# Loading the weights of a one-core network in units of 1 MB with 8192 bytes per row instead of 512 KB with 4096

## The chip, the cores and the metric

The kernel runs on one core of a Trainium2 chip. The metric is the device time of one execution in microseconds (us), taken from the start to the end of the program on the chip. One core has a matrix engine (PE), a vector engine (DVE), an activation engine (ACT), a general engine (POOL), a sequencer that only issues transfers (SP), and 16 DMA engines that move data between the chip's memory (HBM) and the core's own memory (SBUF).

## What is computed

Two networks follow one another on 256 tokens of width 1024, all in float32. The first has two layers: a convolution block and a differential attention, each followed by a mixture of 16 experts of which every token takes 2. The second is one layer: a state-space mixer beside a stick-breaking attention, and a gated feed-forward layer. Cut to the part that the weight loads serve:

```python
def grouped_moe(x, router_w, router_bias, w_gate, w_up, w_down):
    ...
    def step(acc, ew):
        g_e, wg_e, wu_e, wd_e = ew
        h = jax.nn.silu(x2 @ wg_e) * (x2 @ wu_e)
        return acc + (h @ wd_e) * g_e[:, None].astype(x2.dtype), None

    out, _ = lax.scan(step, jnp.zeros_like(x2), (gates.T, w_gate, w_up, w_down))

def first_block(...):
    for l in range(DEPTH):                      # DEPTH = 2
        mix = conformer_conv(...) if l < N_A else diff_attention(...)
        x = layer_norm(ALPHA * x + mix, ln_mix_g[l], ln_mix_b[l])
        ffn = grouped_moe(x, router_w, router_bias, moe_w_gate[l], moe_w_up[l], moe_w_down[l])
        x = layer_norm(ALPHA * x + ffn, ln_ffn_g[l], ln_ffn_b[l])
```

Each layer's experts hold 16 x 3 matrices of 1024 x 512, 96 MB in float32. With the other matrices the program reads some 300 MB of weights, each once.

## The kernel before

The program runs in five phases, one after the other: **A** the convolution block (`pw1`, 8 units of weights, the convolution, `pw2`, 4 units), **B** the first mixture of experts (`moe0`, 96 units), **C** the attention (`wk`, `wq`, `wv`, `wo`, 16 units), **D** the second mixture (`moe1`, 96 units), **E** the second network (`win` 22, `wout` 8, `wup` 22, `wdown` 11 units). A unit is 1 MB: 128 rows (one to each partition of SBUF) of 2048 floats.

**The order of the loads.** All weights go through one list, `plan`, made by `order` (L276) in the order of use, and through one issuing queue, SP's. An entry of the list is a half unit: 128 rows of 1024 floats, 512 KB, rows of 4096 bytes cut from the unit's 8192. `issue` (L299) takes the next entry, takes a slot from a ring and issues the DMA (L304). There are five rings of 512 KB slots, opened as SBUF comes free: `ring1` 6 slots, `ring2` 16, `ring3` 4 and `ring5` 8 (both of `RING3`), `ring4` 4, 38 slots or 19 MB in all. In phase E only `ring1` is left. `half` (L323) hands the next loaded half to the code that uses it and notes its ring; `flush` (L317) issues the next loads once more than `LAG` used halves are noted. An issued load still waits on SP until the last reader of its slot has finished. It waits too until the DMA that last used its completion counter has landed: the program has eight such counters, DMAHW0 to DMAHW7, given in turn to the DMAs of SP and ACT, so that at most eight transfers are under way.

**Phases A, C, E.** `split_half` (L356) splits each half in two: ACT copies it rounded into `wh` (L361), and POOL or DVE, in turn, subtract to get `wl` (L370). `mm3` multiplies three times (L375 to L377). A slot is free when the half's `wl` is done.

**Phases B, D.** The experts go in pairs, p = 0 to 7, 12 units each (gate 4, up 4, down 4). The matmuls read the loaded halves directly: `col2` (L803) issues two matmuls that stand side by side in the array, one for each expert of the pair (L805 and L806). `up` and the down loop (L897) take, for each step, the half `s` of unit `i` and the half `s` of unit `i + 1` (`two_halves`, L808), the first of one expert and the second of the other. `pairs` in `order` lists the halves so: (i, 0), (i+1, 0), (i, 1), (i+1, 1). After the pair p = 0, the code asks whether any expert has got more tokens than its slots hold (`overflow`, L971, the branch at L981); on these inputs none has. All engines, SP too, pass that branch, and at its end SP waits on all eight completion counters before it issues the next load.

**The small transfers of other queues.** At the end of phase D, ACT's queue issues the constants of phase E: `al` and `db` (L1377), `cols_e`, `cst_e`, `cst_eb` (L250) and the meta tokens into `hT` (L1239, pieces of 64 bytes). DVE's first work in phase E is `wdh` (L1303), cast from `cols_e`; the last normalisation of phase D (`v_f` L426, `y` L434) is queued behind it on DVE, and PE's transposes `fm_hT` (L446) need that `y`. PE fills the time with 21 matmuls on a constant (`warm`, L353). Later, in the mixer, SP writes a row to HBM (`acsd`, L1424) and reads it back spread over the partitions (`acs`, L1531) for DVE's `E` (L1538).

Of the kernel before, what the change touches and what calls it, by code (L numbers as in the profile page):

```python
# [9 lines left out]
F32 = mybir.dt.float32  # L10
# [7 lines left out]
P = 128  # L18
# [23 lines left out]
FT = DFF // P  # L42
XT = 12
NEG = -1e30
RING2 = 16
RING3 = (4, 8)
RING4 = 4

W = dict(start=16, a=16, l0=16, lg=9, pos=(4, 6), f0=22, f1=22, l1=18, mix=20)
CONV_PE = (4, 5, 6, 7)  # L50
# [4 lines left out]
LO_DVE = 4  # L55
LO_BOTH = 4
XH_ACT = (1, 2, 3)
LAGS = (6, 2, 2)
M0 = NMETA - 2
NM = L - M0  # L60

# [70 lines left out]
def pack(I):  # L132
    g = {k: np.asarray(v) for k, v in I.items()}
    a = {}
# [4 lines left out]
    c = {}  # L139
# [57 lines left out]
    for l in range(DEPTH):  # L197
        us = []
        for p in range(NE // 2):
            for nm in ("moe_w_gate", "moe_w_up", "moe_w_down"):  # L200
                ua = [units_q(g[nm][l][2 * p + s]) for s in range(2)]
                for h in range(2):
                    us.append(ua[0][h])
                    us.append(ua[1][h])
        a[f"moe{l}"] = np.stack(us)
    order = [0, 4, 1, 5, 2, 6, 3, 7]
    a["wk"] = units_p(g["w_kv"][:, :D], order)
# [15 lines left out]
class Net:  # L223
# [51 lines left out]

    def order(self, phases):  # L276
        plan = []
        add = lambda nm, *ix: plan.extend((nm, i, s) for i in ix for s in range(2))
        pairs = lambda nm: plan.extend((nm, i + e, s) for i in range(0, 96, 2) for s in range(2) for e in range(2))
        if "A" in phases:  # L280
            add("pw1", *range(8))
            add("pw2", *range(4))
        if "B" in phases:
            pairs("moe0")
        if "C" in phases:
            for nm, *ix in (("wk", 0), ("wq", 0), ("wv", 0, 1), ("wk", 1), ("wq", 1), ("wk", 2), ("wq", 2), ("wv", 2, 3), ("wk", 3), ("wq", 3), ("wo", 0, 1, 2, 3)):
                add(nm, *ix)
        if "D" in phases:
            pairs("moe1")
        if "E" in phases:  # L290
            add("win", *range(22))
            add("wout", *range(8))
            add("wup", 0)
            for u in range(FT // 2):
                add("wup", *range(2 * u + 1, min(2 * u + 3, FT)))
                add("wdown", u)
        self.plan = plan

    def issue(self, ring):  # L299
        if self.issued == len(self.plan):  # L300
            return
        nm, i, s = self.plan[self.issued]
        t = self.rings[ring].tile([P, 1024], F32, tag="unit", name=f"u_{nm}_{i}_{s}")
        self.nc.sync.dma_start(t, self.I[nm][i][:, s * 1024:(s + 1) * 1024])  # L304
        self.issued += 1
        self.live.append((nm, i, s, t, ring))
        if self.issued == 1 and nm == "pw1":
            self.first_loads(lambda: self.issue(ring))

    def open_ring(self, ctx, ring, n):  # L310
        self.flush()
# [8 lines left out]
            if r in self.rings and self.issued < len(self.plan) and self.retire.get(r, self.plan[self.issued][0]) == self.plan[self.issued][0]:  # L320
                self.issue(r)

    def half(self, nm, i, s):  # L323
        if not self.live:
            self.flush()
        a, b, c, t, ring = self.live.pop(0)
        assert (a, b, c) == (nm, i, s), (a, b, c, nm, i, s)
        self.used.append(ring)
        self.flush(self.LAG)
        return t  # L330

    def unit(self, nm, i):
        return [self.half(nm, i, s) for s in range(2)]

    def after(self, ins, prev):
        self.tc.add_manual_dep(ins.ins, prev.ins.name, mybir.DependencyInfo(mybir.DependencyClass.NoSync, mybir.DependencyReason.DATA), reason="order")
# [117 lines left out]
    def build(self, phases="ABCDE"):  # L454
        tc, nc = self.tc, self.nc
        self.order(phases)
        with ExitStack() as ctx:
# [14 lines left out]
                self.open_a(late, early)  # L472
            else:
                self.first_loads()
            self.open_ring(ctx, "ring1", 6)
            c2 = ctx.enter_context(ExitStack())
            if phases != "E":
                self.open_ring(c2, "ring2", RING2)
# [17 lines left out]
            if "D" in phases:  # L496
                xs, src = self.moe(1, xs, "mix_g1", "mix_b1", ["ring4", "ring5", "ring3", "ring2"], rows(1))
# [225 lines left out]
    def moe(self, l, n, gname, bname, last_rings, rows):  # L723
        nc = self.nc
        with ExitStack() as ctx:
# [79 lines left out]
                nc.tensor.matmul(ps[0:64], a, ra, start=first, stop=last)  # L805
                self.upped = nc.tensor.matmul(ps[64:128], b, rb, start=first, stop=last)  # L806

            def two_halves(i, s, k):  # L808
                return [self.half(f"moe{l}", i + e, s).rearrange("p (k n) -> p k n", k=k) for e in range(2)]

            def up(p, q, xe, name):
                ps = self.bank(f"{name}{l}{p}")
                for h in range(2):
                    for s in range(2):
                        wa, wb = two_halves(12 * p + 4 * q + 2 * h, s, 2)
                        for kk in range(2):
                            k = 4 * h + 2 * s + kk
                            o = P * (p % 2)
                            col2(ps, xe[:, k, o:o + 64], xe[:, k, o + 64:o + 128], wa[:, kk], wb[:, kk], k == 0, k == KT - 1)
                return ps  # L820
# [34 lines left out]
            for p in range(8):  # L855
# [38 lines left out]
                py = [self.bank(f"py{l}{p}{nh}") for nh in range(2)]  # L894
                for hh in range(2):
                    for kk in range(2):
                        wa, wb = two_halves(12 * p + 8 + 2 * hh, kk, 1)  # L897
                        k = 2 * hh + kk
                        for nh in range(2):
                            s = slice(nh * 512, nh * 512 + 512)  # L900
                            col2(py[nh], hT[:, k, 0:64], hT[:, k, 64:128], wa[:, 0, s], wb[:, 0, s], k == 0, k == 3)
# [69 lines left out]
    def overflow(self, l, b1, xnh, xnl, identr, gname, bname, posm, gates, nmax, xacc):  # L971
        nc, tc = self.nc, self.tc
        units = self.I[f"moe{l}"]

        def chunk(p, i, kk):
            w = self.yy.tile([P, D], F32, tag="yl", name="ovw")[:, :512]
            nc.sync.dma_start(w, units[bass.ds(p * 12 + i, 1), :, kk * 512:(kk + 1) * 512].rearrange("o p n -> p (o n)"))
            return w
# [867 lines left out]
```

## Time and profile before

| | |
|---|---|
| time, median of 3 runs (lowest, highest) | 1196.36 us (1191.97, 1198.35) |
| the profiled execution, its own time | 1195.35 us |
| its span, first to last instruction | 1193.6 us |
| PE, busy share of the span | 96% |
| DVE, ACT, POOL, busy share | 55%, 41%, 27% |
| weight loads on SP's queue | 303.84 MB, 85080 packets |
| PE's granted clock over the span | 0.99 |

The page divides the span into 40 slices of 30 us and gives for each the busy share of every engine and the GB/s that the DMAs moved. Waits are listed by the waiting instruction and by what released it. A matmul's end is modelled from its start, so a matmul that was held up inside the array shows as a longer or as a merged row and counts as busy.

### The profile page before, as it was taken

How to read it: one execution, taken by the hardware profiler on the slowest of the kernel's cores; microseconds unless marked ns; L12 is line 12 of the kernel's file. 1: busy time of each engine (PE TensorE's matmuls, PEld its weight loads, DVE VectorE, ACT ScalarE, POOL GpSimd, SP SyncE). 2: the span in 40 equal slices, each digit the busy share in tenths (PEclk: the TensorE clock that was granted, in tenths of full speed). 3: DMA queues.
4: the chain of work that ended last, by engine and by line, in shares of the span. 5: the costliest groups of instructions: out<-in, count | busy, mean ns of one | idle time of the engine just before them, and what ended most of it. 6: DMA issues, size and time to landing. Idle time of an engine off the chain costs nothing.

```text
span 1193.6 us, 19220 instructions
## 1 busy us (share of the span) xinstructions
PE 1146.7 (96%) x7362; PEld 825.0 (69%) x7370; DVE 652.1 (55%) x1287; ACT 492.1 (41%) x923; POOL 328.1 (27%) x211
## 2 busy tenths in 40 slices
PE   8999899999999999899999998989999998999996
PEld 7998534344335898544344435988999997999996
DVE  5998622222215785632222215974998768655655
ACT  4786311011114575411010114554667666444443
POOL 5872000000002433000000003652222675444443
PEclk8999999999999999999999999999999999999998
DMA  9957498999999866778999996444433463555551
GB/s 350 404 124 223 185 339 330 409 409 409 409 388 347 319 221 214 264 296 328 409 409 409 409 409 210 142 146 150 128 110 101 150 186 116 194 187 180 187 192 46
DMA packets 90214, 311.52 MB, mean 261 GB/s; under 512 B 11215, under 2 KB 14208, under 8 KB 90112
## 3 DMA queue, kind: packets, MB, share of 16 engines
q1 hardware_dynamic: 85080, 303.84, 68.8%
q10 hardware_dynamic: 5032, 6.33, 2.4%
q8 instruction: 62, 1.02, 0.3%
q14 instruction: 40, 0.33, 0.1%
HBM read 307.50 MB, written 2.64 MB: 260 GB/s over the span
## 4 chain that ended last, share of the span: by engine, by line
PE 40%; DVE 8%; ACT 2%; issue 1%; DMA 1%; POOL 1%; ACTq 0%; POOLq 0%; DVEq 0%; SPq 0%
PE py L805 4%; PE up L376 4%; PE up L377 4%; PE up L375 4%; PE pg L805 3%; PE pu L805 3%; PE pdn L377 2%; PE pdn L376 2%; PE pdn L375 2%; DVE E L1538 2%; PE dwin L375 1%; PE dwin L377 1%; PE dwin L376 1%; PE dwout L377 1%; PE dwout L376 1%; PE dwout L375 1%
## 5 line engine op out<-in xcount | busy, mean ns | idle before, releaser
L805 PE MATMUL py<-u_moe,hT 128*64 128x512 f32 x256 | 113.5, 595 | 3.6 <-ACT hT L889 2.6
L805 PE MATMUL pg<-u_moe,xe 128*64 128x512 f32 x256 | 114.6, 594 | 0.0
L806 PE MATMUL py<-u_moe,hT 128*64 128x512 f32 x256 | 114.2, 597 | 0.0
L806 PE MATMUL pu<-u_moe,xe 128*64 128x512 f32 x256 | 113.2, 594 | 0.6 <-DMA u_moe<-in_moe 0.6
L805 PE MATMUL pu<-u_moe,xe 128*64 128x512 f32 x256 | 113.7, 594 | 0.0
L806 PE MATMUL pg<-u_moe,xe 128*64 128x512 f32 x256 | 113.2, 594 | 0.0
L375 PE MATMUL dwin<-xih,wh 128*128 128x272 f32 (+1 forms) x352 | 104.1, 296 | 0.0
L376 PE MATMUL dwin<-xil,wh 128*128 128x272 f32 (+1 forms) x352 | 101.4, 288 | 1.1 <-DVE xil L1279 1.1
L377 PE MATMUL dwin<-xih,wl 128*128 128x272 f32 (+1 forms) x352 | 100.9, 287 | 1.6 <-POOL wl L370 1.6
L376 PE MATMUL up<-fxl,wh 128*128 128x258 f32 (+1 forms) x352 | 99.7, 283 | 1.6 <-DVE fxl L1719 1.6
L874 DVE TENSOR_TENSOR h<-h,pu 128x512 f32<-128x512 f32 x16 | 11.0, 687 | 165.1 <-PE pu L806 151.4
L375 PE MATMUL up<-fxh,wh 128*128 128x258 f32 (+1 forms) x352 | 99.7, 283 | 0.8 <-ACT fxh L1718 0.8
L377 PE MATMUL up<-fxh,wl 128*128 128x258 f32 (+1 forms) x352 | 99.7, 283 | 0.0
L907 DVE SCALAR_TENSOR_TENSOR yl<-py,gc,yh 128x512 fp32r<-128x512 f32 x32 | 23.6, 749 | 108.4 <-ACT yh L906 101.0
L805 PEld LDWEIGHTS py<-u_moe,hT 128*64 128x64 f32 x256 | 33.7, 137 | 71.0 <-issue 61.6
L370 POOL TENSOR_TENSOR wl<-u_win,wh 128x1024 fp32r<-128x1024 f32 x25 | 62.0, 2478 | 63.4 <-ACT wh L361 60.7
L805 PEld LDWEIGHTS pg<-u_moe,xe 128*64 128x64 f32 x256 | 34.1, 137 | 59.0 <-issue 54.2
L370 POOL TENSOR_TENSOR wl<-u_wup,wh 128x1024 fp32r<-128x1024 f32 x22 | 53.6, 2435 | 63.4 <-ACT wh L361 37.4
L805 PEld LDWEIGHTS pu<-u_moe,xe 128*64 128x64 f32 x256 | 34.1, 137 | 52.1 <-issue 50.9
L376 PEld LDWEIGHTS up<-fxl,wh 128*128 128x128 f32 x352 | 66.9, 190 | 2.5 <-DVE fxl L1719 1.8
L375 PEld LDWEIGHTS up<-fxh,wh 128*128 128x128 f32 x352 | 66.9, 190 | 2.0 <-ACT fxh L1718 1.3
L376 PEld LDWEIGHTS dwin<-xil,wh 128*128 128x128 f32 x352 | 66.3, 188 | 2.0 <-DVE xil L1279 1.9
(537 smaller groups left out, 3237.5 us busy)
## 6 DMA issues: line engine op xcount, KB each, us to landing
u_moe<-in_moe SPq DMA_DIRECT2D x384, 512.0 KB, 10.2
u_win<-in_win SPq DMA_DIRECT2D x44, 512.0 KB, 3.6
u_wup<-in_wup SPq DMA_DIRECT2D x44, 512.0 KB, 4.0
u_pw<-in_pw SPq DMA_DIRECT2D x24, 512.0 KB, 10.2
u_wdown<-in_wdown SPq DMA_DIRECT2D x22, 512.0 KB, 4.0
u_wout<-in_wout SPq DMA_DIRECT2D x16, 512.0 KB, 3.8
u_wk<-in_wk SPq DMA_DIRECT2D x8, 512.0 KB, 7.3
u_wq<-in_wq SPq DMA_DIRECT2D x8, 512.0 KB, 9.3
```

The source lines that it names most:

```text
L370: eng.tensor_tensor(l, w, h.bitcast(F32), ALU.subtract)
L375: mm(ps, lh, rh, start=first, stop=False)
L376: mm(ps, lh, rl, start=False, stop=False)
L377: mm(ps, ll, rh, start=False, stop=last)
L805: nc.tensor.matmul(ps[0:64], a, ra, start=first, stop=last)
L806: self.upped = nc.tensor.matmul(ps[64:128], b, rb, start=first, stop=last)
L874: nc.vector.tensor_tensor(h, h, pu, ALU.mult)
L907: nc.vector.scalar_tensor_tensor(yl[:, s], py[nh], gc, yh[:, s].bitcast(F32), op0=ALU.mult, op1=ALU.subtract)
L1538: nc.vector.tensor_scalar(E[:, q:q + w], a[:, i, q:q + w], nA[:, c, h:h + 1], 0.0, op0=ALU.add, op1=ALU.min)
```

## The change

- A load is one DMA of a whole unit, 1 MB, 128 rows of 8192 bytes. `issue` takes a tile of [128, 2, 1024]; `unit` hands out its two halves.
- The rings have half as many slots of twice the size: 3, 8, 2 and 4, 2, so 19 slots and the same 19 MB. `LAGS` goes from (6, 2, 2) to (3, 1, 1), in units now.
- The expert weights are packed anew in HBM: a unit holds one step's half of one expert and, in the same row, that of the other. `moe0` and `moe1` are then listed plainly, unit 0 to 95, and `both` replaces `two_halves`.
- The very first unit is still loaded in two DMAs with the input `xT` between them; the second unit of `pw1` now follows at once, ahead of `cols_a` and the other constants.
- The overflow code, which does not run, finds its pieces at the new places.

```diff
-LAGS = (6, 2, 2)
+LAGS = (3, 1, 1)
...
                 for h in range(2):
-                    us.append(ua[0][h])
-                    us.append(ua[1][h])
+                    for c in (slice(0, 1024), slice(1024, 2048)):
+                        us.append(np.concatenate([ua[0][h][:, c], ua[1][h][:, c]], 1))
...
-        nm, i, s = self.plan[self.issued]
-        t = self.rings[ring].tile([P, 1024], F32, tag="unit", name=f"u_{nm}_{i}_{s}")
-        self.nc.sync.dma_start(t, self.I[nm][i][:, s * 1024:(s + 1) * 1024])
+        nm, i = self.plan[self.issued]
+        t = self.rings[ring].tile([P, 2, 1024], F32, tag="unit", name=f"u_{nm}_{i}")
+        src = self.I[nm][i].rearrange("p (s n) -> p s n", s=2)
         self.issued += 1
-        self.live.append((nm, i, s, t, ring))
+        self.live.append((nm, i, t, ring))
         if self.issued == 1 and nm == "pw1":
-            self.first_loads(lambda: self.issue(ring))
+            self.nc.sync.dma_start(t[:, 0], src[:, 0])
+            self.first_loads(lambda: (self.nc.sync.dma_start(t[:, 1], src[:, 1]), self.issue(ring)))
+        else:
+            self.nc.sync.dma_start(t, src)
...
-            def two_halves(i, s, k):
-                return [self.half(f"moe{l}", i + e, s).rearrange("p (k n) -> p k n", k=k) for e in range(2)]
+            def both(i, k):
+                return [w.rearrange("p (k n) -> p k n", k=k) for w in self.unit(f"moe{l}", i)]
```

At the branch on SP's queue (L981 before, L982 after), half a unit moves. Before, in the list of `moe0`:

```order
L304 DMA u_moe0_30_0_2056<-in_moe0 128x1024
L304 DMA u_moe0_31_0_2058<-in_moe0 128x1024
L304 DMA u_moe0_30_1_2064<-in_moe0 128x1024
L981 COMPARE_AND_BRANCH
...
L981 UNCONDITIONAL_BRANCH
L304 DMA u_moe0_31_1_2066<-in_moe0 128x1024
L304 DMA u_moe0_32_0_2072<-in_moe0 128x1024
```

and after:

```order
L311 DMA u_moe0_30_1973<-in_moe0 128x2048
L311 DMA u_moe0_31_1979<-in_moe0 128x2048
L982 COMPARE_AND_BRANCH
...
L982 UNCONDITIONAL_BRANCH
L311 DMA u_moe0_32_1985<-in_moe0 128x2048
L311 DMA u_moe0_33_1991<-in_moe0 128x2048
```

The last load ahead of the branch was the third of four halves of a pair of units; now the pair is whole, and the branch stands between two pairs.

On SP's queue in phase E, around the write of `acsd` and its read `acs0`, before:

```order
L304 DMA u_win_7_1_7640<-in_win 128x1024
L304 DMA u_win_8_0_7726<-in_win 128x1024
L1424 DMA acsd_7589<-acs_row_7587 16x258
L1531 DMA acs0_8152<-acsd_7589 128x516
L304 DMA u_win_8_1_7728<-in_win 128x1024
L1531 DMA acs1_8182<-acsd_7589 128x516
```

and after:

```order
L311 DMA u_win_7_7185<-in_win 128x2048
L1425 DMA acsd_7136<-acs_row_7134 16x258
L1532 DMA acs0_7687<-acsd_7136 128x516
L311 DMA u_win_8_7271<-in_win 128x2048
L1532 DMA acs1_7717<-acsd_7136 128x516
```

The half of unit 8 that stood ahead of `acsd` now goes with the other, behind `acs0`.

On ACT in phase A, where `sg0` is the gate of the first result and `dg0` are diagonal matrices for the convolution, made from `wch` and `wcl`, before:

```order
L361 ACTIVATE wh_232<-u_pw1_0_1_120 128x1024
L604 ACTIVATE dg0_0_386<-cst_m_126,wch_197 128x128 x3
L604 ACTIVATE dg0_0_386<-cst_m_126,wcl_198 128x128 x4
L361 ACTIVATE wh_265<-u_pw1_1_0_132 128x1024
L645 ACTIVATE sg0_261<-pw1_0_207,cols_a_122 128x256
L361 ACTIVATE wh_294<-u_pw1_1_1_134 128x1024
```

and after:

```order
L361 ACTIVATE wh_211<-u_pw1_0_114 128x1024
L361 ACTIVATE wh_244<-u_pw1_1_121 128x1024
L361 ACTIVATE wh_273<-u_pw1_1_121 128x1024
L645 ACTIVATE sg0_240<-pw1_0_186,cols_a_123 128x256
L604 ACTIVATE dg0_0_365<-cst_m_127,wch_176 128x128 x3
L604 ACTIVATE dg0_0_365<-cst_m_127,wcl_177 128x128 x4
```

The seven `dg0` copies moved from before the second unit's splits to behind `sg0`.

## Rows read from the trace of the kernel before

**Rows 1.** The page: GB/s moved in 40 slices of 30 us

```profile
GB/s 350 404 124 223 185 339 330 409 409 409 409 388 347 319 221 214 264 296 328 409 409 409 409 409 210 142 146 150 128 110 101 150 186 116 194 187 180 187 192 46
```

**Rows 2.** Waits, all engines: who waited for what, us in total, times, longest

```profile
PEld py L805 <- DMA u_moe<-in_moe: 5.5, 14, 1.9
DVE wdh L1303 <- DMA cols_e<-in_cols_e: 2.9, 1, 2.9
DVE E L1538 <- DMA acs<-acsd: 2.3, 1, 2.3
```

**Rows 3.** Waits of SP's queue, same columns

```profile
SPq L304 <- DMA u_moe<-in_moe: 258.9, 279, 3.9
SPq L981 <- SPq L981: 21.4, 6, 10.7
```

**Rows 4.** Timeline of PE, end of phase B: start, us, what, [idle before it]

```profile
344.27 0.64 PE L806 MATMUL pu<-u_moe,xe 128*64 128x512 f32 x1
...
349.51 1.07 PE L805 MATMUL pu<-u_moe,xe 128*64 128x512 f32 x2
...
359.00 1.88 PE L805 MATMUL py<-u_moe,hT 128*64 128x512 f32 x4
...
363.41 1.50 PE L805 MATMUL py<-u_moe,hT 128*64 128x512 f32 x3 [1.04 <-DMA u_moe<-in_moe]
...
366.62 1.52 PE L828 MATMUL sum<-yh,sT 128*128 128x512 f32 x4
```

**Rows 5.** Timeline of PE, the same stretch of phase D

```profile
705.40 0.64 PE L806 MATMUL pu<-u_moe,xe 128*64 128x512 f32 x1
...
723.01 1.37 PE L828 MATMUL sum<-yh,sT 128*128 128x512 f32 x4
```

**Rows 6.** Stretches: PE, PEld, DVE, ACT, POOL busy, PEclk, DMA share, GB/s

```profile
180.00:210.00 30.00, 27.76 (x142) 12.47 (x138) 7.03 (x12) 4.54 (x9) 0.00 (x0) 1.00 0.87 330
210.00:240.00 30.00, 30.00 (x154) 11.28 (x155) 6.66 (x14) 2.92 (x5) 0.00 (x0) 1.00 1.03 409
330.00:360.00 30.00, 29.42 (x127) 11.04 (x124) 4.20 (x8) 3.54 (x5) 0.00 (x0) 1.00 1.01 379
```

**Rows 7.** One DMA queue, whole span and 937.1 to 938.1 us: packets, MB, share

```profile
q14 instruction: 40, 0.33, 0.1%
...
q14 instruction: 1, 0.01, 1.9%
```

**Rows 8.** Timelines of ACT's queue, DVE and PE, from phase D to E

```profile
724.27 0.34 ACTq L250 DMA_DIRECT2D cols_e<-in_cols_e  x1
...
727.25 0.21 DVE L424 BATCH_NORM_AGGREGATE mv_f<-st_f 128x2 f32<-128x12 f32 x1
730.34 0.23 DVE L1303 CAST wdh<-cols_e 128x128 fp32r<-128x128 f32 x1 [2.88 <-DMA cols_e<-in_cols_e]
...
725.15 4.96 PE L353 MATMUL warm<-warm_b 128*128 128x512 bf16 x21
733.05 3.42 PE L446 MATMUL fm_hT<-cst_m,y 128*128 128x128 f32 x16 [2.94 <-DVE y L434]
```

**Rows 9.** A stretch within that change of phase, columns as in rows 6

```profile
726.00:728.00 2.00, 2.00 (x11) 0.88 (x10) 1.43 (x5) 0.00 (x0) 0.00 (x0) 1.00 0.94 175
```

**Rows 10.** Phase A: what the engines waited for from 4 to 30 us

```profile
DVE hp L646 <- ACT sg L645: 3.6, 1, 3.6
PE pw L377 <- DVE wl L368: 0.3, 1, 0.3
```

**Rows 11.** DMA issues (KB each, us to landing), and one refill in phase E

```profile
u_moe<-in_moe SPq DMA_DIRECT2D x384, 512.0 KB, 10.2
u_wup<-in_wup SPq DMA_DIRECT2D x44, 512.0 KB, 4.0
...
1036.70 0.33 SPq L304 DMA_DIRECT2D u_wup<-in_wup  x1
...
1045.64 1.06 ACT L361 ACTIVATE wh<-u_wup 128x1024 fp32r<-128x1024 f32 x1 [1.71 <-PE up L376]
```

More of the change, by code (lines that the diff above doesn't have):

```diff
@@ L44 @@
 NEG = -1e30
-RING2 = 16
-RING3 = (4, 8)
-RING4 = 4
+RING1 = 3
+RING2 = 8
+RING3 = (2, 4)
+RING4 = 2
 W = dict(start=16, a=16, l0=16, lg=9, pos=(4, 6), f0=22, f1=22, l1=18, mix=20)
@@ L277, in order @@
         plan = []
-        add = lambda nm, *ix: plan.extend((nm, i, s) for i in ix for s in range(2))
-        pairs = lambda nm: plan.extend((nm, i + e, s) for i in range(0, 96, 2) for s in range(2) for e in range(2))
+        add = lambda nm, *ix: plan.extend((nm, i) for i in ix)
         if "A" in phases:
@@ L283, in order @@
         if "B" in phases:
-            pairs("moe0")
+            add("moe0", *range(96))
         if "C" in phases:
@@ L288, in order @@
         if "D" in phases:
-            pairs("moe1")
+            add("moe1", *range(96))
         if "E" in phases:
@@ L321, in flush, with unit @@
                 self.issue(r)
-    def half(self, nm, i, s):
+    def unit(self, nm, i):
         if not self.live:
             self.flush()
-        a, b, c, t, ring = self.live.pop(0)
-        assert (a, b, c) == (nm, i, s), (a, b, c, nm, i, s)
+        a, b, t, ring = self.live.pop(0)
+        assert (a, b) == (nm, i), (a, b, nm, i)
         self.used.append(ring)
         self.flush(self.LAG)
-        return t
-    def unit(self, nm, i):
-        return [self.half(nm, i, s) for s in range(2)]
+        return [t[:, s] for s in range(2)]
     def after(self, ins, prev):
@@ L474, in build @@
                 self.first_loads()
-            self.open_ring(ctx, "ring1", 6)
+            self.open_ring(ctx, "ring1", RING1)
             c2 = ctx.enter_context(ExitStack())
@@ L814, in up @@
                     for s in range(2):
-                        wa, wb = two_halves(12 * p + 4 * q + 2 * h, s, 2)
+                        wa, wb = both(12 * p + 4 * q + 2 * h + s, 2)
                         for kk in range(2):
@@ L896, in moe @@
                     for kk in range(2):
-                        wa, wb = two_halves(12 * p + 8 + 2 * hh, kk, 1)
+                        wa, wb = both(12 * p + 8 + 2 * hh + kk, 1)
                         k = 2 * hh + kk
@@ L975, in chunk @@
         def chunk(p, i, kk):
+            i, kk = i - i % 2 + kk // 2, i % 2 * 2 + kk % 2
             w = self.yy.tile([P, D], F32, tag="yl", name="ovw")[:, :512]
```

## The prediction

> **What bounds the kernel now.** I read the GB/s by slice first, then the waits, then the timelines where the waits sit. PE is busy nearly all the time, so an edit to loads can only pay where PE stands for a load. The slices show two plateaus at exactly 409 GB/s, the greater part of the two expert phases, and far less in the second network [rows 1]. On the plateau the DMA engines are the limit: SP is held back 279 times by a load that has not landed [rows 3], and their busy share is full [rows 6]. So the expert phases live on the 19 MB that were loaded ahead, and run out of them at their end.
>
> The list of waits hides this. It charges PE's weight loads only 5.5 us in 14 pieces [rows 2]. But a matmul's end is modelled, so a late load shows as one long merged row: 1.88 us for four matmuls, and so on [rows 4]. The honest measure is the same work twice. From one given `pu` matmul of the last expert pair to its first `sum`, phase B takes 366.62 - 344.27 = 22.35 us [rows 4] and phase D 723.01 - 705.40 = 17.61 us [rows 5]. **Phase B loses 4.74 us at its end** to late loads. In phase D the loads come just in time.
>
> The second place is the change from phase D to E. The last loads of `moe1` and the first three units of `win` are still under way when ACT asks for `cols_e` at 724.27. DVE is free at 727.25 + 0.21 = 727.46, waits for `cols_e` until 730.34, and holds the last normalisation behind it; PE then stands for 2.94 us before `fm_hT` [rows 8]. In the middle of that stretch the DMA engines are 94% busy and move 175 GB/s [rows 9]: they are full, and with small pieces.
>
> **The change, part by part.**
>
> *Rows of 8192 bytes.* On the plateau each of 16 engines moves 409 / 16 = 25.6 GB/s, so 8192 bytes, now two packets, take 0.320 us. The trace has a few packets of 0.33 MB / 40 = 8.2 KB on another queue; one of them, alone in a window of 1 us, took 1.9% of 16 engine-microseconds, 0.304 us, which rounding leaves between 0.296 and 0.312 [rows 7]. With nothing else, that is a gain of 2.5 to 7.5%; with something added for the update of the counter, or if it is HBM or the path that limits, it is nothing. I bound it by 0 and 5% and take 3%, since the packet on record is nearest in kind.
>
> What 3% gives: 64 units are loaded after the branch in each expert phase, 64 x 1.049 MB / 409 GB/s = 164 us, of which 3% are 4.9 us. Some 13 units load back to back ahead of the branch, which adds 1.0 us. So the last unit lands about **5.9 us earlier**, and each per cent is worth 2.0 us. Phase B needs 4.74, that is 2.4%. I enter **-4.7**. In phase D nothing is lost now but a tenth here or there: **-0.2**.
>
> *The branch.* In the 30 us that hold it, 330 GB/s were moved and not 409 [rows 6]: 79 x 30 / 409 = 5.8 us of loading are lost, since SP waits 10.7 us for eight counters [rows 3] and the queue then refills from nothing. After the change the same eight counters are awaited, the data ahead of them is one half unit more, and the refill is as long. The half unit, 0.5 MB / 409 = 1.3 us, only moves from behind the branch to ahead of it. Entry 0; bounds 1.3 us of lead either way, which in phase B is a gain or loss of at most that. The same holds for twice as much data under way: on a plateau that is already full a longer queue adds no rate.
>
> *From D to E.* If all weight loads are 5.9 us ahead, the first three `win` units, which ended near 730 us, end near 724, when `cols_e` is only being asked for. Then `wdh` starts when DVE is free, 2.88 us earlier. PE's `warm` ends at 725.15 + 4.96 = 730.11, and `fm_hT` would come at 733.05 - 2.88 = 730.17, so no new floor is in the way [rows 8]. What is late next is `cst_e`, asked for right after `cols_e` and needed by DVE within 1.5 us of `wdh`; for it I keep 0.2 back. Entry **-2.7**, bounds 0 and -2.9.
>
> What the trace shows there is that small pieces beside weight packets make slow progress. [...]
>
> *Issue order in phase E.* Ahead of `acsd` one half unit fewer is issued, so `acs0`, for which DVE waits 2.3 us [rows 2], meets less traffic. PE has other matmuls there; entry **-0.3**, bounds 0 and -1.0.
>
> *Whole units in the ring of three.* A unit's slot comes free when its second half is split, and its first split now needs all of it. In the tightest refill the second half is issued at 1036.70 and the unit's first split begins at 1045.64, 8.94 us later [rows 11]. A half lands in 4.0 us there [rows 11]; eight more packets per engine at 0.16 us make 5.3 (an estimate from these rows). That leaves 3.6 us, so entry 0. [...]
>
> *Phase A.* The second unit overtakes `cols_a`, so that ACT's splits come sooner and the `dg0` copies after `sg0`. PE's listed waits there are tenths: 0.3 us for a `wl` [rows 10]. The copies now stand between `sg0` and the third unit's splits and can delay those by as much. Entry 0, bounds -0.5 and +0.5. The halved count of issues on SP costs nothing: SP has been waiting for landings, not for its own issuing.
>
> **The sum**, against the profiled execution's 1195.35 us: -4.7 - 0.2 - 2.7 - 0.3 = -7.9, so 1187.4. The profiled execution stands 1.0 us below the median of the runs, 1196.36; the same ratio gives 1188.4. I say 1188.
>
> **The rivals.**
>
> *The rate does not rise.* For it: the plateau is so flat that something other than packets may set it. Against it: in the trace a packet of twice the size takes less than twice the time. Then phase B's end and the wait for `cols_e` stay, and only -0.3 and the tenths of phase A remain: 1195, and to 1197 if the constants' pieces wait longer between larger packets: `cols_e` has 128 rows, 8 to an engine, and 8 x 0.15 us make 1.2.
>
> *Half of it.* The lead comes, but the wait at the change of phase passes from `cols_e` to `cst_e` or the meta tokens, or the lead is 1.5% and covers 3 us of phase B. One term or the other falls: 1190 to 1192.
>
> *Slower: the ring of three starves.* Place: the splits of phase E, a slot freed only as a whole. It decides from a landing time of 8.94 us on. For it: the expert loads took 10.2 us from issue to landing [rows 11], which is over that. Against it: they had seven others ahead of them, and in phase E hardly half of the rate is used [rows 1]. If a unit took 10.2 us, each of the ten repeated groups of three units would start 10.2 - 8.9 = 1.3 us late, 13 us in all: 1188 + 13 = 1201.
>
> **How the numbers follow.** The forecast gets 0.55: the packet on record carries it. The flat rate gets 0.27, half of it 0.08, the starving ring 0.10. A measurement of this kernel can tell about 0.5% from no change, 6 us, so the bound lies at 1190.4. The forecast's bounds, -10.5 to -6, fall on the faster side; of the half case a quarter does: 0.57 faster. The flat rate and the rest of the half case are within the bound: 0.33. Slower: 0.10. The range runs from 1185, all terms at their good ends, to 1196.5, which takes in most of the flat-rate case and leaves out the starving ring.
>
> **What would show it.** Slices of the plateaus at about 421 GB/s, with packets of 8192 bytes on the weights' queue (half as many of them). The stretch from the `pu` matmul to `sum` in phase B at 17.6 us, as in phase D. `wdh` no longer waiting for `cols_e`, and `fm_hT` right behind `warm`. No new wait of ACT's splits for `u_wup` or `u_wdown`. If the slices stay at 409, the step on packets is wrong and with it the two main terms; if they rise and the stretch stays at 22 us, it was not the loads that held PE there.

## The result and the profile after

| | before | after |
|---|---|---|
| time, median of 4 runs (lowest, highest) | 1196.15 us (1191.97, 1198.35) | 1176.18 us (1173.67, 1177.86) |
| the profiled execution, its span | 1195.35, 1193.6 us | 1173.67, 1171.9 us |

The ratio is 0.9836, with a 95% interval of 0.9819 to 0.9852: 20 us less, where the prediction said 8 and its range ended at 1185. The sign was right and so was the mechanism that the prediction named; a second one, of about the same size, was missing from it.

The page of the changed kernel, GB/s by slice of 29.3 us and the DMA packets (to be held against [rows 1]):

```profile
GB/s 357 415 108 253 179 365 362 421 420 423 420 408 377 318 154 215 252 378 369 422 420 422 421 420 116 136 181 118 116 101 109 153 221 76 216 180 159 202 195 57
DMA packets 49603, 311.48 MB, mean 266 GB/s; under 512 B 6703, under 2 KB 9696, under 8 KB 13408
q1 hardware_dynamic: 44472, 303.82, 65.9%
```

Three stretches of the same kernel, columns as in [rows 6]:

```profile
180.00:210.00 30.00, 27.76 (x150) 12.79 (x148) 7.53 (x14) 4.51 (x8) 0.00 (x0) 1.00 0.89 365
210.00:240.00 30.00, 30.00 (x152) 11.74 (x148) 7.32 (x15) 2.36 (x4) 0.00 (x0) 1.00 1.01 421
330.00:360.00 30.00, 29.89 (x141) 12.34 (x141) 7.93 (x20) 4.87 (x8) 0.00 (x0) 1.00 0.93 376
```

The plateaus rose from 409 to 421 GB/s, which is 2.9%; 3% was forecast. In the stretch of the branch (the first of the three) 365 GB/s are moved where it was 330. From 200 to 212 us into the two expert phases 313 and 331 GB/s are moved, where it was 345 and 409: the expert loads are through early. In B the last unit of `moe0` lands 205.2 us after the first `pg` matmul, where it was 217.3.

The end of phase B on PE (columns as in [rows 4]) is now a chain of plain pairs, L805 and L806 side by side every 0.43 us, with no merged row left:

```profile
336.23 0.59 PE L805 MATMUL pu<-u_moe,xe 128*64 128x512 f32 x1
336.25 0.59 PE L806 MATMUL pu<-u_moe,xe 128*64 128x512 f32 x1
...
353.46 0.59 PE L805 MATMUL py<-u_moe,hT 128*64 128x512 f32 x1
353.47 0.59 PE L806 MATMUL py<-u_moe,hT 128*64 128x512 f32 x1
354.05 0.73 PE L828 MATMUL sum<-yh,sT 128*128 128x512 f32 x2
```

The L806 at 336.25 begins the `pu` matmul with which [rows 4] begin (344.27). To the first `sum` it is 354.05 - 336.25 = 17.80 us here and was 22.35; the residual sums, 1.1 us that stood ahead of it before, now lie inside.

The change from D to E, on ACT's queue, DVE and PE (columns as in [rows 8]):

```profile
706.04 0.39 ACTq L251 DMA_DIRECT2D cols_e<-in_cols_e  x1
...
708.75 0.21 DVE L424 BATCH_NORM_AGGREGATE mv_f<-st_f 128x2 f32<-128x12 f32 x1
709.64 0.23 DVE L1304 CAST wdh<-cols_e 128x128 fp32r<-128x128 f32 x1 [0.69 <-DMA cols_e<-in_cols_e]
...
706.79 4.96 PE L353 MATMUL warm<-warm_b 128*128 128x512 bf16 x21
712.20 2.16 PE L446 MATMUL fm_hT<-cst_m,y 128*128 128x128 f32 x16 [0.44 <-DVE y L434]
```

`cols_e` is waited for 0.69 us instead of 2.88, and PE's idle time in front of `fm_hT` fell from 2.94 to 0.44. From 706 to 708 us the DMA engines are 31% busy, where in the middle of this stretch they were 94% busy before [rows 9].

**Where the time went.** The table gives the length of each stage in the profiled executions, from starts of matmuls that both kernels have. Phases B and D are counted from the first `pg` to the last `sum`.

| stage, us | before | after | difference |
|---|---|---|---|
| A and the rest ahead of B's first `pg` | 147.40 | 144.60 | -2.8 |
| B | 221.28 | 211.48 | -9.8 |
| C, to D's first `pg` | 140.20 | 139.03 | -1.2 |
| D | 216.03 | 211.44 | -4.6 |
| D to E, last `sum` to `fm_hT` | 8.14 | 5.65 | -2.5 |
| E, with the end of the program | 462.30 | 461.47 | -0.8 |
| whole execution | 1195.35 | 1173.67 | -21.7 |

Two lines stand out against the sum of the prediction: B has twice what was entered, and D, for which 0.2 was entered, has 4.6. B and D are now equally long to 0.04 us: after the change both run at PE's own pace. PE and its weight loads wait 2.5 us in all for expert weights, where it was 13.5.

### The profile page after: what moved, and what is told of

The parts are those of the page before. It is cut to its first block, busy times and chain, and to the rows that moved or that the text cites. A ratio compares the mean times of both kernels' runs of the same rounds, so it can differ in the third digit from the quotient of the medians.

```text
span 1171.9 us, 18667 instructions
## 1 busy us (share of the span) xinstructions
PE 1130.2 (96%) x7362; PEld 816.3 (70%) x7370; DVE 652.1 (56%) x1287; ACT 492.5 (42%) x923; POOL 327.1 (28%) x211
## 4 chain that ended last, share of the span: by engine, by line
PE 40%; DVE 7%; ACT 3%; issue 1%; POOL 1%; DMA 0%; ACTq 0%; DVEq 0%; POOLq 0%
PE py L805 4%; PE up L376 4%; PE up L377 4%; PE up L375 4%; PE pg L805 3%; PE pu L805 3%; PE pdn L377 2%; PE pdn L376 2%; PE pdn L375 2%; DVE E L1539 2%; PE dwin L375 2%; PE dwin L376 2%; PE dwin L377 2%; PE dwout L377 1%; PE dwout L376 1%
## 5 line engine op out<-in xcount | busy, mean ns | idle before, releaser
L805 PE MATMUL py<-u_moe,hT 128*64 128x512 f32 x256 | 113.3, 595 | 2.6 <-ACT hT L889 2.6
L805 PE MATMUL pg<-u_moe,xe 128*64 128x512 f32 x256 | 114.2, 594 | 0.0
L806 PE MATMUL pg<-u_moe,xe 128*64 128x512 f32 x256 | 113.7, 593 | 0.0
L806 PE MATMUL py<-u_moe,hT 128*64 128x512 f32 x256 | 113.3, 595 | 0.0
L805 PE MATMUL pu<-u_moe,xe 128*64 128x512 f32 x256 | 113.1, 593 | 0.0
L806 PE MATMUL pu<-u_moe,xe 128*64 128x512 f32 x256 | 113.1, 593 | 0.0
L375 PE MATMUL dwin<-xih,wh 128*128 128x272 f32 (+1 forms) x352 | 104.1, 296 | 1.1 <-DVE xih L1279 1.1
L375 PE MATMUL up<-fxh,wh 128*128 128x258 f32 (+1 forms) x352 | 100.5, 285 | 0.8 <-ACT fxh L1719 0.8
L805 PEld LDWEIGHTS py<-u_moe,hT 128*64 128x64 f32 x256 | 33.7, 137 | 71.8 <-issue 68.0
L805 PEld LDWEIGHTS pg<-u_moe,xe 128*64 128x64 f32 x256 | 34.3, 137 | 60.4 <-issue 55.5
L805 PEld LDWEIGHTS pu<-u_moe,xe 128*64 128x64 f32 x256 | 34.4, 137 | 59.0 <-issue 57.9
L375 PEld LDWEIGHTS up<-fxh,wh 128*128 128x128 f32 x352 | 67.6, 192 | 2.0 <-ACT fxh L1719 1.3
L361 ACT ACTIVATE wh<-u_wup 128x1024 fp32r<-128x1024 f32 x44 | 46.4, 1059 | 51.6 <-PE up L376 48.5
```

Source lines behind the costliest of these rows:

```text
L361: c = nc.scalar.activation(h, w, AF.Copy)
L375: mm(ps, lh, rh, start=first, stop=False)
```

## The experiments

Line numbers in the runs below are shifted by a few lines where the edit added some; the measured ratios are to the kernel before, run in the same series.

### The changed kernel again

> The changed kernel again, unedited, as the reference for the runs beside it. Both theories: 1176 us (1173.5 to 1178.5). Its first 20 us are looked at for the granted clock: in the two profiles so far the PE idles 1.83 us after the first matmul in both, and then the clock was 0.50 for 6 us before and 1.00 after, which is worth 2.8 us. If that is chance, repeats of the same kernel will show both; if the new order of the first loads sets it, all of them will show 1.00.

> The changed kernel once more, unedited, as the reference for the three runs beside it: 1178 us (1175 to 1180). Its profile is the third one of this kernel; the stages of phase B and D are expected to repeat to 0.1 us, those before and after them to vary by 1 to 2 us.

Measured: 1178.77 us, ratio 0.9844 (0.9824 to 0.9864), just above what was expected, and 1177.31 us, 0.9836 (0.9817 to 0.9854). Beside the kernel before in the same series that is 17.0 and 19.6 us less by the medians. B is 211.51 and 211.49, D 211.45 in both, so the two expert phases repeat to 0.1 us. A's gain over the profile of before is 1.5 us in both and not 2.8, and C was 139.4 and 141.3. A and C scatter from one execution to the next, and the profiled execution of after had luck in both.

### Where D's 4.6 us come from: a change of PE's order that the prediction left out

D had hardly a late load to lose, so its gain needed another cause. It stands in the order of PE, at the second column matmul of expert pair p = 5. Before:

```
L805 MATMUL pg05_3163<-u_moe0_60_0_2889,xe02_2911 64x512
L796 MATMUL pst05_3196<-cst_m_126,S02_2908 128x128 x2
L799 MATMUL pst05_3196<-gates0_1860,S02_2908 64x1 x4
L806 MATMUL pg05_3163<-u_moe0_61_0_2891,xe02_2911 64x512
```

and after:

```
L805 MATMUL pg05_2984<-u_moe0_60_2746,xe02_2764 64x512
L806 MATMUL pg05_2984<-u_moe0_60_2746,xe02_2764 64x512
L805 MATMUL pg05_2984<-u_moe0_60_2746,xe02_2764 64x512
L806 MATMUL pg05_2984<-u_moe0_60_2746,xe02_2764 64x512
L796 MATMUL pst05_3009<-cst_m_127,S02_2761 128x128 x2
```

Before, the two matmuls of a step read two loads, and the scheduler put whatever else was ready between them: `pst` of p = 5 and 6, and twice the residual sums (L852) of p = 7. That is four places in each expert phase. Now both matmuls read one load and come ready together, so the other work stands behind the pairs. One float32 matmul of the program stands in the trace as two records: the four of L799 above are `x8` below. What such a place costs is in the timeline of PE, first of before, at the same place of p = 6, with the two records of a lone L805 in one row:

```profile
307.27 1.02 PE L805 MATMUL pg<-u_moe,xe 128*64 128x512 f32 x2
308.23 0.44 PE L796 MATMUL pst<-cst_m,S 128*128 128x128 f32 x2
308.59 0.41 PE L799 MATMUL pst<-gates,S 128*64 128x1 f32 x8
308.85 0.62 PE L805 MATMUL pg<-u_moe,xe 128*64 128x512 f32 x1
308.86 0.62 PE L806 MATMUL pg<-u_moe,xe 128*64 128x512 f32 x1
309.31 0.59 PE L805 MATMUL pg<-u_moe,xe 128*64 128x512 f32 x1
```

and then of after:

```profile
304.06 0.59 PE L805 MATMUL pg<-u_moe,xe 128*64 128x512 f32 x1
304.06 0.59 PE L806 MATMUL pg<-u_moe,xe 128*64 128x512 f32 x1
304.49 0.59 PE L805 MATMUL pg<-u_moe,xe 128*64 128x512 f32 x1
304.49 0.59 PE L806 MATMUL pg<-u_moe,xe 128*64 128x512 f32 x1
304.92 0.59 PE L805 MATMUL pg<-u_moe,xe 128*64 128x512 f32 x1
304.92 0.59 PE L806 MATMUL pg<-u_moe,xe 128*64 128x512 f32 x1
305.45 0.44 PE L796 MATMUL pst<-cst_m,S 128*128 128x128 f32 x2
```

Two records side by side take 0.43 us, so a pair of matmuls takes 0.86; one matmul alone takes about as long, 0.96 us from 307.27 to 308.23. A split shifts the pairing: one matmul runs alone at the split, and one later, where the pairs come together again (for p = 5 and 6 at the end of `pu`). Two run alone where one pair would have done, so a place costs some 0.9 us. From this came **theory 1**: a phase ends at the later of two chains, PE's own, which the split pairs lengthen by some 3.7 us, and that of the loads. **Theory 2**, the rival, was that only the loads count. Three kernels tell them apart.

**The changed kernel with the split pairs put back.** Loads as after, PE's order as before:

```diff
-            def col2(ps, a, b, ra, rb, first, last):
-                nc.tensor.matmul(ps[0:64], a, ra, start=first, stop=last)
+            def col2(ps, a, b, ra, rb, first, last, mid=None):
+                i = nc.tensor.matmul(ps[0:64], a, ra, start=first, stop=last)
+                if mid:
+                    i0, i1 = mid()
+                    self.after(i0, i)
                 self.upped = nc.tensor.matmul(ps[64:128], b, rb, start=first, stop=last)
+                if mid:
+                    self.after(self.upped, i1)
...
+                pg = up(p, 0, xe, "pg", first if p == 7 else (lambda: slots(p, st)) if p in (5, 6) else None)
...
+                pu = up(p, 1, xe, "pu", (lambda: residual(1, *parts)) if p == 7 else None)
```

> The changed kernel with the split pairs put back: the transposes pst of the expert pairs 5 and 6 and the residual sums of pair 7 stand between the first and the second matmul of a pair, as the kernel before had them; loads of 8192-byte rows stay. Theory 1: the loads are ahead, so PE's own chain sets the end and each of the 8 places costs 0.83 us: 1176 + 6.6 = 1182.6 (1181 to 1184). Rival (the split pairs cost nothing, all was late loads): 1176 (1174 to 1178).

Measured: 1185.36 us, 0.9908 (0.989 to 0.9925), 6.6 us more than the changed kernel in the same series, which is the difference expected (the time itself is above the expected range, as that kernel's was). B is 215.17 and D 215.09, each 3.7 us longer, for four places, 0.92 us each. Its timeline shows the row of before again:

```profile
304.53 1.02 PE L807 MATMUL pg<-u_moe,xe 128*64 128x512 f32 x2
305.48 0.44 PE L796 MATMUL pst<-cst_m,S 128*128 128x128 f32 x2
```

**The kernel before with whole pairs.** The reverse: loads as before, the other work ordered behind the pair.

```diff
+                    i0 = nc.tensor.transpose(pt[:, tb * P:(tb + 1) * P], ...)
+                    if p > 4:
+                        self.after(i0, self.upped)
...
-                    nc.tensor.matmul(sums[tb][nh], identr, xh[:, s], start=True, stop=False)
+                    self.after(nc.tensor.matmul(sums[tb][nh], identr, xh[:, s], start=True, stop=False), self.upped)
```

> The kernel before with one thing taken from the changed one: the transposes pst of the expert pairs 5 and 6 and the residual sums of pair 7 come behind whole pairs of half-array matmuls and no longer between the two of a pair; loads as before, 512 KB in rows of 4096 bytes. It takes away 8 split pairs, each worth 0.83 us of PE time by the comparison of the two traces. Theory 1: the loads set the ends of both phases, so PE only waits longer for them: 1194 to 1197, against 1196 before. Theory 2 (terms add up): 1196 - 6.6 = 1189.5 (1188 to 1191).

Measured: 1196.65 us, 1.0003 (0.9987 to 1.0018): nothing. B is 220.51, D 217.72 (1.7 longer than before) and the way from D to E 10.30 (2.2 longer). PE gets through the pairs sooner and then stands for loads, as the waits of PE's weight loads say (columns as in [rows 2]; with the smaller rows and PE's own waits it is 24.8 us for expert weights in all, and 13.5 before):

```profile
PEld pg L808 <- DMA u_moe<-in_moe: 8.2, 8, 1.1
PEld pu L808 <- DMA u_moe<-in_moe: 4.7, 6, 1.5
PEld pg L807 <- DMA u_moe<-in_moe: 3.5, 14, 0.3
PEld py L807 <- DMA u_moe<-in_moe: 3.5, 8, 1.7
```

The largest two rows are those of L808, the second matmul of a pair: its half unit lands after that of the first. So the order by itself is worth 0 us with the old loads and 6.6 us with the new ones. Both chains have to become shorter; the change shortens both.

**The new units, but rows of 4096 bytes.** The units lie in HBM as two blocks of 128 rows, and one DMA of 1 MB fetches both.

```diff
-        src = self.I[nm][i].rearrange("p (s n) -> p s n", s=2)
+        src = self.I[nm][i]
+        src = bass.AP(tensor=src.tensor, offset=src.offset, ap=[[1024, P], [1024 * P, 2], [1, 1024]])
```

> The changed kernel with one thing undone: each 1 MB load reads 256 pieces of 4096 bytes (the unit is packed in HBM as two blocks of 128 x 1024) instead of 128 of 8192. Slots, issue order, counters and PE's order stay. Theory 1 (the ends of both expert phases are the later of two chains, PE's own and the loads' at the plateau rate): the plateaus fall from 421 to 409 GB/s, phase B's last unit lands some 8 us after PE could use it, phase D's some 4, and the wait for cols_e returns, 2.5: 1176 + 15 = 1191 (1188 to 1194). Theory 2 (the gain is PE's order and the larger DMAs, the packet size is not needed): 1176 (1174 to 1179).

Measured: 1183.13 us, 0.9884 (0.9865 to 0.9903): between the two numbers expected and in neither range. The plateau is back at 409 GB/s, where rows of 8192 bytes gave 421 with DMAs of the same 1 MB, so here the rate hangs on the length of the rows, not on the size of a DMA:

```profile
GB/s 347 404 118 256 171 363 352 409 409 409 409 405 409 311 151 197 266 325 355 409 410 408 409 409 179 140 170 140 102 125 107 143 184 119 199 183 156 211 188 61
```

But B is 215.64 and D 213.55, where the same rate with 512 KB loads and whole pairs gave 220.51 and 217.72. Larger DMAs do something for the loads beside the rate. The prediction had said that they do not.

### What larger DMAs give

Phase B's last whole slice in [rows 1] (388, from 328 to 358 us) is below the plateau before the loads are through; the kernel with 4096-byte rows holds 405 there. From 200 to 212 us into the phase the kernel before moves 345 GB/s (columns as in [rows 6]):

```profile
347.40:359.40 12.00, 11.42 (x47) 4.41 (x44) 1.17 (x3) 0.39 (x1) 0.00 (x0) 1.00 0.98 345
```

The waits of SP's queue from 325 to 370 us of the kernel before name a cause that the prediction passed over:

```profile
SPq L304 <- DMA u_moe<-in_moe: 22.6, 17, 3.9
SPq L304 <- DMA bt<-vecd: 6.9, 2, 4.7
```

`bt` is a tile of biases for phase C, of which ACT's queue loads two ahead of time (L1094, at 342.54 and 343.12 us). Each takes one of the eight completion counters that SP and ACT share, in turn. SP, which issues the last unit of `moe0` only at 354.5 us, waits for those counters while the 512 KB loads under way run out. So one kernel loads `bt` after phase B:

```diff
-            nc.scalar.dma_start(bt, ...)
+            self.after(nc.scalar.dma_start(bt, ...), self.scaled)
```

> The kernel before with one thing moved: the two bias loads bt that ACT issues near the end of phase B, 256 KB each in short pieces, are issued after phase B instead. SP waited 6.9 us for their counters there while its own loads ran low. Theory 1b: the loads of phase B's last five units land some 3 us earlier, phase B takes 218 us from its first pg matmul to its last sum instead of 221.3, total 1196 - 3 = 1193. Rival (the rate alone sets the landing; bt is small): 221, total 1196.

Measured: 1191.45 us, 0.9957 (0.9937 to 0.9976). B is 216.28, 5.0 us less, where 3 had been expected, and D as before (215.84). SP's wait for `bt` is gone from the same stretch, and from 200 to 212 us into B the rate stays up:

```profile
346.40:358.40 12.00, 12.00 (x55) 5.06 (x52) 1.18 (x3) 0.38 (x1) 0.00 (x0) 1.00 1.03 407
```

Of the 5.0 us, some 1.1 need not be `bt`'s: in the stretch of the branch this kernel moved 346 GB/s over 30 us and the kernel before 331, (346 - 331) x 30 / 409, and `bt` comes long after. Still, this is the kernel before with a single line moved: some half to two thirds of the late loads in B (2.8 to 3.9 of 6.1 us) were two small transfers in the wrong place.

The changed kernel leaves `bt` where it was, and SP waits for it longer, from 325 to 366 us:

```profile
SPq L311 <- DMA bt<-vecd: 16.0, 1, 16.0
```

It costs B nothing there, since the last unit of `moe0` is issued at 333.6 us, ahead of `bt` at 336.6: the wait falls on the loads of phase C.

**Both, whole pairs and `bt` late**, to see what 512 KB loads at 409 GB/s can do at best:

> The kernel before with both edits of the two earlier runs: no split pairs, and the bt loads put behind phase B. PE's own chain is then 211.5 us in each expert phase, so what is left over that is late loads at 409 GB/s in units of 512 KB. Theory (the larger transfers gave phase B only what the bt loads had cost SP's queue, some 4.5 us, and the width of the rows the rest): the last unit lands as in the kernel with bt late (210.6 us into the phase), and phase B is 215.0 to 216.3 us, as with 1 MB transfers of 4096-byte rows (215.6); phase D as with whole pairs alone, 217 to 218; the time about 1191, the same as with bt late alone, since whole pairs again give nothing where the loads are late. Rival (larger transfers also raise the rate on the way): phase B is 217.5 us or more. Second rival (PE's chain was the limit with bt late, not the loads): phase B falls to 212 to 213.5 and the time to 1187.

Measured: 1192.12 us, 0.9968 (0.9956 to 0.9981), the same as with `bt` late alone. B is 217.70 and D 215.77. Beside whole pairs alone (220.51) that is 2.8 us less for `bt`, where the run before had 5.0; and B came out 1.4 us above what the theory said and just inside its rival's bound. D, for which 217 to 218 was expected, came out 1.95 us shorter than with whole pairs alone, though `bt` is not loaded there. Against 1 MB loads at the same rate (215.64 and 213.55) there are 2.1 us left in B and 2.2 in D, which `bt` does not explain. One place where the loads differ is the branch. From 30 to 60 us into phase B, the stretch of the branch, the 1 MB loads with 4096-byte rows move (last column, GB/s)

```profile
175.41:205.41 30.00, 27.76 (x142) 12.58 (x140) 7.04 (x12) 4.51 (x8) 0.00 (x0) 1.00 0.90 353
345.41:357.41 12.00, 10.29 (x46) 4.09 (x48) 1.17 (x3) 0.39 (x1) 0.00 (x0) 1.00 1.03 403
```

and the kernel with whole pairs and `bt` late

```profile
176.23:206.23 30.00, 27.76 (x142) 12.59 (x140) 7.04 (x12) 4.50 (x8) 0.00 (x0) 1.00 0.89 333
346.23:358.23 12.00, 11.79 (x51) 5.33 (x52) 1.17 (x3) 0.38 (x1) 0.00 (x0) 1.00 1.03 407
```

The second row of each is the stretch from 200 to 212 us into the phase, where the two are alike. In B, 20 GB/s over 30 us are (353 - 333) x 30 / 409 = 1.5 us, and the 20 us ahead of it give 1.1 more (410 against 388 GB/s); in D it is 1.2 (356 against 340) and 0.3 (405 against 398). That is about the size of what is left, but it is not shown to be the cause. This stretch scatters from run to run (333 and 346 GB/s in B of the two kernels with `bt` late), so that a single phase that waits for loads is known to 1 or 2 us only, as D shows above. And the trace of the kernel with whole pairs and `bt` late has something else in pair p = 7 that the 1 MB loads don't have:

```profile
329.75 1.04 PE L807 MATMUL pg<-u_moe,xe 128*64 128x512 f32 x2
330.93 0.64 PE L808 MATMUL pg<-u_moe,xe 128*64 128x512 f32 x1
...
339.51 1.02 PE L808 MATMUL pg<-u_moe,xe 128*64 128x512 f32 x2
...
362.09 1.31 PE L830 MATMUL sum<-yh,sT 128*128 128x512 f32 x4 [0.71 <-ACT yh L908]
```

The first matmul of the pair starts alone, as its half unit is there and the other is not, so late loads split the pairs that the order had made whole; it happens once more in `pu`, and in both again in D. At some 0.9 us for a place, and 0.7 and 0.8 us of waiting for `yh` ahead of the first `sum`, this too is enough for the 2.1 us (an estimate from these rows). No run separates the two. Nor is it known what fills the branch's gap better with 1 MB loads, if they do: the amount under way, the size of one DMA, or the half unit that moves ahead of the branch, 1.3 us by the prediction's own bound.

**A test that failed.** To tell the amount under way from the size, each unit was loaded in two DMAs of 64 rows of 8192 bytes:

```diff
-            self.nc.sync.dma_start(t, src)
+            for q in (slice(0, 64), slice(64, 128)):
+                self.nc.sync.dma_start(t[q], src[q])
```

> The changed kernel with rows of 8192 bytes, but each unit is loaded by two DMAs of 64 rows, so that a DMA is 512 KB again and the eight counters hold 4 MB under way, not 8. Pairs stay whole. Theory 1b (two things sped up the loads: the larger packets, worth 6 us at the end of phase B, and twice as much data under way, worth some 4.5 there, because the queue refills faster after the branch and rides over the constants that ACT loads): plateaus at 421 GB/s, phase B's last unit some 4.5 us later than in the changed kernel, where 1.9 us were to spare: phase B 2 to 3 us longer, phase D 0 to 1, total 1178 + 3 = 1181. Theory 1a (only the packet size matters): 1178, as the changed kernel.

Measured: 1590.22 us, 1.3293 (1.3261 to 1.3325), where both theories expected about 1180. It says nothing on the question, since the DMAs of 64 rows move at 218 GB/s, where those of 128 rows gave 421. The page:

```profile
DMA  9997999999999999999999999999666547678874
GB/s 219 225 202 152 219 225 236 218 215 217 218 219 225 232 228 208 207 220 229 241 220 216 218 216 218 219 221 225 143 151 144 122 97 160 143 162 180 180 171 106
q1 hardware_dynamic: 48984, 303.84, 86.8%
```

The DMA engines are full at 218 GB/s, and PE, which now waits for loads in both expert phases, is busy for 79% of the span at a granted clock of 0.904.

### The two scattered places: phase A and the change to E

Phase A came out 2.8, 1.5 and 1.5 us shorter in three executions of the changed kernel, 2.0 us with 4096-byte rows, and 1.0 to 1.2 us in the three kernels with the old loads above, whose phase A was not touched. The windows of PE's granted clock (the last column but two) show why. Before:

```profile
8.00:12.00 4.00, 2.17 (x11) 2.14 (x11) 4.00 (x6) 3.25 (x6) 2.39 (x4) 0.63 1.05 389
12.00:16.00 4.00, 4.00 (x21) 4.00 (x21) 0.97 (x2) 2.62 (x7) 3.21 (x4) 0.51 1.03 410
```

and the profiled execution of after:

```profile
8.00:12.00 4.00, 2.17 (x18) 2.02 (x18) 4.00 (x6) 2.85 (x4) 1.12 (x2) 1.00 1.03 420
12.00:16.00 4.00, 4.00 (x36) 4.00 (x35) 2.05 (x3) 2.10 (x3) 4.00 (x6) 1.00 1.06 414
```

PE idles for 1.83 us in front of its second real matmul, waiting for DVE's `xl`, in both kernels. In the first the clock falls to half behind that, in the second it does not, and the changed kernel again had 0.79 and 0.79 in one execution, 0.69 and 0.88 in another. The three kernels with the old loads lie between as well (0.74 to 0.84 in the first window). Among executions with a clock in between, A is 145.94 us in the changed kernel and 146.2 to 146.4 with the old loads, so by this comparison the change itself gives A some 0.3 to 0.5 us and the clock the rest. So one kernel fills that idle time with nine matmuls on a constant, and puts three of DVE's casts for phase E (`wdh` among them) behind the last normalisation of D:

```diff
+                    m0 = nc.tensor.matmul(pb[:, s], wh[:, k], xh[:, k], start=True, stop=False)
+                    pw = self.bank("warm")
+                    for _ in range(9):
+                        m0 = self.after(nc.tensor.matmul(pw, self.warm_b, ...), m0)
...
-        nc.vector.tensor_copy(wdh, wd)
+        self.after(nc.vector.tensor_copy(wdh, wd), self.normed)
```

> The changed kernel with two small additions, as a try for a faster one. PE gets 9 filler matmuls where it idles 1.83 us after its first product, and the three casts of phase E's constants on DVE come behind the normalisation of phase D instead of before it. If the low clock after that idle is what costs up to 2.8 us in some executions, those disappear and the runs draw together; the casts should give 1 us. Expected 1175 (1173 to 1177), the spread of the runs smaller. Rival (the clock falls and rises for other reasons, and the casts are needed anyway): 1178, no change.

Measured: 1176.12 us, 0.9824 (0.9806 to 0.9843); the changed kernel in the same series had 1177.31. A is 3.1 us shorter than before, and the way from D to E 5.04 us, 0.55 less than there. Its five runs lie between 1175.49 and 1176.18, all below the five of the changed kernel (1176.57 to 1177.93). In its trace PE's clock stays at 1.00 from 8 to 16 us. E came out 0.9 us longer than there, so 1.1 us of the 2.2 are left in the traces, and the two additions were not run apart. It is the fastest version that was run, by about 1.2 us, though the lowest single run of the changed kernel (1173.67) is still below it.

## Why the prediction was wrong

The forecast lacks 12 of the 20 us. 7.3 of them are the order of PE, to which the prediction gave nothing without saying why; some 2.1 are late loads beyond the 4.9 entered for B and D; the rest is phase A and scatter. The signs that it had named came true or nearly so (421 GB/s, a stretch of 17.8 us, a short wait for `cols_e`, no starving ring): none of them looks at the order on PE.

**The packets: right.** 409 to 421 GB/s is the 3% that was chosen between 0 and 5, and rows of 4096 bytes bring 409 back. With 1 MB loads the last unit of `moe0` lands 211.6 us into the phase in rows of 4096 bytes and 205.2 to 206.6 in rows of 8192: 5.0 to 6.4 us earlier, where 5.9 was worked out. The two kernels differ by 4.2 us in B and 2.1 in D; PE's chain hides the rest.

**The end of phase B: right in its place, too small.** Entered: -4.7. With the split pairs still there, B loses its late loads and goes from 221.28 to 215.17, which is -6.1. The yardstick was off: phase D was taken as free of late loads, and it lost 216.03 - 215.09 = 0.9 us to them itself.

**"On a plateau that is already full a longer queue adds no rate": a step that failed.** The sentence is true of the plateau (409 GB/s with 512 KB and with 1 MB) and was used for all of the phase. Beside the rows, the larger loads bring B's last unit from 217.3 to 211.6 us, 5.7 us for which 0 was entered. Most of it is `bt`: moving that alone gives 212.2, 5.1 us less, or 3.3 less beside whole pairs alone. It is a row of SP's queue that the prediction did not read, since it looked at the queue for the loads alone. What 1 MB loads give beyond `bt`, some 2 us in each phase, is open between the branch and the halves that land one after the other. The 5.9 us alone would not have freed B of late loads: once the pairs are whole, PE asks for the last unit some 4 us earlier.

**The order on PE: the step that failed most, by being left out.** The split pairs cost 3.7 us in each expert phase, 7.3 in all, and the prediction gave the new packing no effect on PE. The row was there to be read: a merged row of two records of one matmul at 307.27 us, in the middle of a phase, far from the end of its loads. Of D's -4.6, 3.7 are this and 0.9 late loads, where -0.2 was entered.

**From D to E: right.** Entered -2.7, measured -2.5 to -2.6 in three executions, against one trace of the kernel before (8.14 us); the other three kernels with the old loads took 9.5 to 10.3 there, so this term too is known to 1 or 2 us only. `cols_e` meets hardly any weights now (the DMA engines are 31% busy from 706 to 708 us), so no run shows what small pieces pay beside packets of 8192 bytes, nor the 1.2 us that the prediction put on it in its first rival; what the runs show there is the wait for `cols_e`, 2.88 us before and 0.69 after.

**The row `acs`: right in sign.** Entered -0.3. From the hundredth `dwin` matmul of L375 to `vt` it is 7.22 us before and 5.74, 6.86 and 5.84 after: -0.4 to -1.5, and the bound was -1.0.

**Ring of three: right.** No wait of ACT's splits for `u_wup` or `u_wdown` appeared; a unit of `wup` landed in 5.3 us, as estimated, and E is as long as before but for 0.8 us.

**Phase A: the entry 0 was wrong for a reason that is no part of the change.** Of the gain of 1.5 to 2.8 us all but some 0.3 to 0.5, by the comparison above, depends on the clock in the executions compared. With the idle time filled it is 3.1 us in the one trace, and the five runs spread over 0.7 us, those of the changed kernel beside them over 1.4.

**The rivals.** The flat rate, half the effect and the starving ring all failed. The rival that was missing is the one that came true: the change makes PE's own chain shorter. Added up with what the runs showed, loads first and then the order: late loads -7.0 (B 6.1, D 0.9), split pairs -7.3, D to E -2.5, E with `acs` -0.5 to -0.8, phase A -1.5 to -2.8, gives -18.8 to -20.4; the medians differ by 20.0, and by 17.0 and 19.6 in the two repeats. What is left in the profiled executions, -21.7, is C, which lies between 139.0 and 142.1 us in the kernels run here with no pattern that was found.

## What to carry to other kernels

A change to how data is loaded also tells the scheduler when things come ready, so compare the order on the engine that sets the pace, and price each place where it moves, even if the count of instructions is the same. A phase ends at the later of the compute chain and the load chain: shortening one alone can measure as nothing, as whole pairs did without the new loads (1.0003), and shortening both can give more than the sum. Two operands of one step that come in two loads can also land apart and split the step again. Read the loading queue's waits for transfers of other queues too: two small loads that share the completion counters cost B some 3 to 4 us (2.8 and 5.0 in two comparisons), nearly as much as the rate of the packets (4.2).

## What the runs showed of the hardware

- Rows of 8192 bytes, each one packet, move at 421 GB/s on the plateau, rows of 4096 bytes at 409: from 210 to 240 us SP's queue moves 12.61 MB in 1730 packets after, 191 of them under 512 bytes, and 12.26 MB in 3371 before, 379 of them under 512. For rows of 4096 bytes it made no difference on the plateau whether a DMA had 512 KB or 1 MB (409 GB/s in both).
- A DMA of 64 rows of 8192 bytes, with the engines full, gets 218 GB/s; with 128 rows it gets 421. Packets of the same size take nearly twice as long: from 210 to 240 us SP's queue has the 16 engines fully busy in both kernels and moves 6.77 MB here, 12.61 MB in the changed kernel. Each unit is two such DMAs in this run, one for partitions 0 to 63 and one for 64 to 127, and 218 GB/s is the rate of both together. What holds it there is not shown.
- Two half-array matmuls side by side take 0.86 us, two records of 0.43 each, and one alone about as long: the merged row at 307.27 us holds PE for 0.96. A place where other work stands between the two costs 0.92 us (8 places, 7.3 us).
- Behind the same idle time of about 1.83 us PE's granted clock fell to 0.51 in one execution (12 to 16 us) and stayed at 1.00 in another. The changed kernel itself differs from one execution to the next (1.00, 0.79 and 0.69 from 8 to 12 us). Why it falls in one execution and not in another is not shown.
